# A hybrid decoder layer: the samples' token tile with high and low parts side by side, jobs moved two tiles ahead, and two unread matmuls behind each row of 1/rms

## The chip, the core and the metric

The kernel runs on one core of one Trainium2 chip. The metric is device time in microseconds. Five engines of the core appear in the text: TensorE (PE, with its weight loads PEld), VectorE (DVE), ScalarE (ACT), GpSimd (POOL) and SyncE (SP), which issues most of the DMAs. PSUM, which TensorE writes, is used in banks of 512 fp32 columns.

## The reference

One decoder layer is run for a prompt of 1024 tokens and for 8 sequences of 8 sample tokens (64 samples), with the same weights, 1024 model columns and fp32 data. Cut to the parts that matter here:

```python
def layer(x, ...):
    h = rmsnorm(x, norm_mix)                       # x / sqrt(mean(x*x) + EPS) * g
    q, k, v, gu, gv, ga, gb = split_in(h @ w_in)   # 1024, 256, 256, 768, 768, 1024, 1024 columns
    o, nk, nv = attn_prompt(...) or attn_sample(...)     # window of 128
    vn = layernorm(jax.nn.gelu(gv), ln_g, ln_b)
    s = spatial_gating(jax.nn.gelu(gu), vn, ws, bs)
    merged = jax.nn.sigmoid(ga) * (o @ w_pa) + jax.nn.sigmoid(gb) * (s @ w_pb)
    x = x + merged @ w_out
    f, nconv = conv_ffn(rmsnorm(x, norm_ffn), w_up, conv_w, conv_b, w_down, conv_prev)
    return x + f, nk, nv, nconv, vn
```

A final RMSNorm follows. This text is about the first tenth of the run: h, and of the projection the columns of v and gv.

## The kernel before

**Split numbers.** Every fp32 operand of a large product is split into a high part, which fp32r holds exactly, and a low part, the rest (`split`, L39; `scale_split`, L43, which also scales by the norm's gains). A product is hi·hi + hi·lo + lo·hi: three matmuls into one PSUM bank for each of eight chunks (k) of 128 model columns. A split is a ScalarE copy (L40, L44) and a VectorE subtraction (L41, L45).

**Tokens.** They stand in two groups. Group 0 holds the tile "s" of the 64 samples and the prompt's tiles 0 to 3 (576 tokens), group 1 tiles 4 to 7 (512 tokens). In the first stage, the token stage, the tokens' h is the stationary operand (128 rows of it) and 256 columns of the weights are the moving one, so that the result has tokens as rows: `mm_tok` (L527, matmul L531), 24 matmuls a tile. The samples' tile takes 128 rows as well: 64 samples and the first 64 of prompt tile 0, whose results nobody reads there.

**Order of the token stage.** There are four blocks of 256 columns: gv0, gv1, gv2 and v. Their weights (`w2h`, `w2l`) have two buffers. First comes gv0 for group 0, chunk by chunk as x and weights arrive, into five banks (120 matmuls). Then `tokens` (L570) runs through whole tiles: gv1, v and gv2 for group 0, five tiles each, then v, gv2, gv0 and gv1 for group 1, four tiles each: 31 tiles of 24 matmuls. After that the other columns are computed with weights stationary and tokens moving (`product`, L290, matmul L300), 288 tokens at a time for group 0 and 256 for group 1. These are the products that fill the middle of the run.

**1/rms.** Group 0's h is used without 1/rms, which is applied to the results by row (`rstg`, L537 and L567). The sum of squares by column, `rsg`, is made by ScalarE's squares (L616, L645, L648) and VectorE's additions (L618, L637). `stats` (L470) adds it up over the partitions with fp32 matmuls of one column (L475), takes the root (`rroot`, L255: VectorE, then POOL), and spreads it on diagonals (L482 on ScalarE, L484 on VectorE). `rows` (L486) turns the diagonals into rows by fp32 matmuls with ones (L492) and copies them to `rsg` (L495). For group 1, 1/rms goes into h itself (`norm1`, L661), for which the rows are needed.

**Jobs.** After each tile `tokens` pops one function of the list `jobs` (L717) and runs it. So the list says behind which tile the work of VectorE and ScalarE for later is written: the rows of group 0, group 1's four pairs of squares (`squares1`), `stats1`, the rows of group 1 with the first of four `norm1`, then the sums and splits that the products need (`sums1`, `sums0`, `split0`). A scheduler then sets the final order on each engine from what depends on what.

**Results and room.** `v_out` (L534) and `gv_out` (L564) take a tile from PSUM through ScalarE (L537, the gelu L567) and send it out; gv goes to a DRAM buffer on ScalarE's DMA queue (L568). Group 0's h stands in the space of `txa[0]`, the split tokens of the products (`h_of`, L517); its part `txa[0][3]` stays free until `split0(3)`. Later the LayerNorm over gv reads each tile back (`ln_load`, L743; `ln_stats`, L754; `ln_out`, L764), the samples' tile with 128 rows like the others.

Of the kernel before, what the change touches and what calls it, by code (L numbers as in the profile page):

```python
# [15 lines left out]
P = 128  # L16
# [18 lines left out]
def layer(tc, a):  # L35
# [11 lines left out]
    with ExitStack() as top:  # L47
# [310 lines left out]
        with ExitStack() as ph1:  # L358
# [108 lines left out]
            def bank():  # L467
                return psa.tile([P, 512], F32, name="st")

            def stats(g):  # L470

                acc, n = rsg[g], groups[g]["n"]
                pt = (bank() if g else bank5[4])[:, 256:256 + len(groups[g]["toks"])]
                for i, (_, lo) in enumerate(groups[g]["toks"]):
                    PE.matmul(pt[:, i:i + 1], acc[:, lo:lo + P], ones[:, 0:1], start=True, stop=True)  # L475
                rroot(rstg[g], pt)

                dg = stage(n)
                for i, (name, lo) in enumerate(groups[g]["toks"]):
                    m = NS if name == "s" else P  # L480
                    if g:
                        S.activation(dg[0:m, lo:lo + m], ident[0:m, 0:m], AF.Copy, scale=rstg[g][0:m, i:i + 1])  # L482
                    else:
                        V.tensor_scalar(dg[0:m, lo:lo + m], ident[0:m, 0:m], rstg[g][0:m, i:i + 1], None, ALU.mult)  # L484

                def rows():  # L486
                    ps, at = None, 512
                    for name, lo in groups[g]["toks"]:
                        m = NS if name == "s" else P
                        if at + m > 512:  # L490
                            ps, at, lo0 = bank(), 0, lo
                        PE.matmul(ps[:, at:at + m], ones[0:m], dg[0:m, lo:lo + m], start=True, stop=True)  # L492
                        at += m
                        if at + P > 512 or lo + m == n:
                            S.copy(acc[:, lo0:lo + m], ps[:, :at])  # L495
                return rows

            pa0, th0, pa = ExitStack(), ExitStack(), ExitStack()
# [28 lines left out]
            def mm_tok(ps, g, lo, w, k):  # L527
                wh, wl = w
                ah, al = ((part1(t, k, lo) for t in txa[1][k % 4]) if g else (t[:, lo:lo + P] for t in hs[k]))
                for i, (u, v) in enumerate(((ah, wh), (ah, wl), (al, wh))):  # L530
                    PE.matmul(ps, u, v[:, k, :], start=k + i == 0,  # L531
                              stop=k == KD - 1 and i == 2)

            def v_out(g, i, ps):  # L534
                name = groups[g]["toks"][i][0]
                v = gvp.tile([P, 256], F32, name="gv")
                S.activation(v, ps, AF.Copy, scale=1.0 if g else rstg[g][:, i:i + 1])  # L537
                if name == "s":
                    nc.sync.dma_start(vsd, v[0:NS])
                    for b in range(8):  # L540
                        nc.sync.dma_start(a["vsn"][b], v[8 * b:8 * b + 8])
                else:
                    if name == 4:
                        late["v"] = gvp.tile([P, 256], F32, name="gv")
                        nc.sync.dma_start(late["v"], v3d)
                    for to, x in ((vd, v), (dvd, None)):
                        if x is None and name == 0:
                            continue
                        t = W.sm.tile([P, 4, P], F32, name="ws", bufs=2)
                        tr, four = t.bitcast(F32R), lambda y: y.rearrange("p (h d) -> p h d", d=64)  # L550
                        if x is None:
                            x = t[:, :, 64:128]
                            V.tensor_sub(x, four(v), four(late["v"]))
                            scale_split(tr[:, :, 0:64], tr[:, :, 64:128], x, sign)
                        else:
                            split(tr[:, :, 0:64], tr[:, :, 64:128], four(x))
                        nc.sync.dma_start(to[name], t)
                    late["v"] = v
                    if name == 3:
                        nc.sync.dma_start(v3d, v)  # L560
                if name == 7:
                    nc.sync.dma_start(a["vp"], v)

            def gv_out(g, i, p3, ps, v=None):  # L564
                if v is None:
                    v = gvp.tile([P, 256], F32, name="gv")
                S.activation(v, ps, AF.Gelu_apprx_tanh, scale=1.0 if g else rstg[g][:, i:i + 1])  # L567
                nc.scalar.dma_start(gvd[groups[g]["toks"][i][0]][:, 256 * p3:256 * p3 + 256], v)  # L568

            def tokens(g, key, out, jobs, new=True, after=None):  # L570
                if new:
                    W.get()
                    W.get()
                for i, (_, lo) in enumerate(groups[g]["toks"]):
# [168 lines left out]
            def ln_load(n):  # L743
                if n < len(lnn):
                    if "lnp" not in late:
                        lnp = late["lnp"] = poola("ln", 1, lno)
                        for x in ("lng", "lnb"):
                            late[x] = lnp.tile([P, GW], F32, name=x)
                            nc.sync.dma_start(late[x], a[x])
                    g, i = lnn[n]  # L750
                    lnv[n] = late["lnp"].tile([P, GW], F32, name="v", bufs=4)
                    nc.sync.dma_start(lnv[n], gvd[groups[g]["toks"][i][0]])

            def ln_stats(n):  # L754
                lnp, v = late["lnp"], lnv[n]
                bs_ = lnp.tile([P, 2, 6], F32, name="bst", bufs=2)
                for e in range(2):
                    V.bn_stats(bs_[:, e], v[:, e * 384:e * 384 + 384])
                mv = lnm[n] = lnp.tile([P, 3], F32, name="mv", bufs=3)
                V.bn_aggr(mv[:, 0:2], bs_)  # L760
                V.tensor_scalar(mv[:, 2:3], mv[:, 1:2], EPS, None, ALU.add)
                G.tensor_tensor(mv[:, 2:3], mv[:, 2:3], mhalf[:, 0:1], ALU.pow)

            def ln_out(n):  # L764
                (g, i), v, mv = lnn[n], lnv.pop(n), lnm.pop(n)
                V.scalar_tensor_tensor(v, v, mv[:, 0:1], late["lng"], ALU.subtract, ALU.mult)
                V.scalar_tensor_tensor(v, v, mv[:, 2:3], late["lnb"], ALU.mult, ALU.add)
                nc.sync.dma_start(vnd[g][:, :, i], v.rearrange("p (g c) -> p g c", c=P))
                if groups[g]["toks"][i][0] == "s":
                    nc.sync.dma_start(a["gvs"], v[0:NS])  # L770

            def ln_half(n, e):
                def go():
# [1227 lines left out]
```

## Time and profile before

| | |
|---|---|
| median of 3 runs | 1510.91 us (1510.36 to 1510.93) |
| profiled execution | 1509.93 us, of which the span is 1508.2 |
| granted TensorE clock | 0.998 |
| TensorE busy | 1493.7 us, 99% of the span, 12190 matmuls |
| VectorE, ScalarE, POOL busy | 1158.7 (77%), 825.9 (55%), 265.8 (18%) us |
| first product of the next stage | at 112.44 us |

A timeline row of the trace gives start, time covered, engine, line, operation, result<-operands, partitions, shapes and how many instructions follow one another in it; a time in brackets at its end is the engine's idle time before it and what ended it. A matmul's time covered is longer than its distance to the next one, since they are pipelined; the distance is read from the starts. A row of a window gives the window, its length, then busy time and count for TensorE, its loads, VectorE, ScalarE and POOL, then clock, DMA share and GB/s. Rows of the engines' order have no times: they give line, operation, result<-operands and the count of equal ones in a row.

### The profile page before, as it was taken

Reading aid. Unit: us, or ns where it says so; the run is one execution under the profiler, and the core shown is the slowest. Engines: PE = TensorE matmul, PEld = TensorE weight load, DVE = VectorE, ACT = ScalarE, POOL = GpSimd, SP = SyncE. Lnnn points to the kernel's source line nnn. Section 1 sums busy time; section 2 is a strip of 40 time slices with the busy share of each in tenths; the row PEclk is TensorE's granted clock in tenths of the full one; section 3 lists DMA queues with packets and bytes.
Section 4 is the critical chain, followed back from the end, with each engine's and each line's share of the span. In section 5 each row is a group of like instructions: output and inputs, shape, how many; then the busy total and the mean of one; then the engine's idle time right before and its main releaser. Section 6 shows DMA issues by size and latency. Waiting matters only on the chain.

```text
span 1508.2 us, 31375 instructions
## 1 busy us (share of the span) xinstructions
PE 1493.7 (99%) x12190; PEld 1481.7 (98%) x12190; DVE 1158.7 (77%) x1909; ACT 825.9 (55%) x1755; POOL 265.8 (18%) x422
## 2 busy tenths in 40 slices
PE   9999999999999999999999999999999999999997
PEld 9999999999999999999999999999999999999997
DVE  6896778756645995989668888898899888785685
ACT  6665764544543774874434555555555556453463
POOL 0000012200120331530222322322132122000002
PEclk9999999999999999999999999999999999999999
DMA  8452457637749757849978333332233226973453
GB/s 289 157 188 112 179 177 265 228 126 271 243 167 333 249 181 224 254 160 322 342 257 282 129 115 122 117 117 107 98 136 109 91 74 219 367 259 97 123 183 133
DMA packets 137508, 286.70 MB, mean 190 GB/s; under 512 B 15248, under 2 KB 44368, under 8 KB 137360
## 3 DMA queue, kind: packets, MB, share of 16 engines
q1 hardware_dynamic: 132352, 279.97, 55.2%
q10 hardware_dynamic: 5008, 4.73, 0.9%
q8 instruction: 96, 1.57, 0.4%
q14 instruction: 52, 0.43, 0.1%
HBM read 195.76 MB, written 90.85 MB: 190 GB/s over the span
## 4 chain that ended last, share of the span: by engine, by line
PE 76%; DVE 5%; ACT 2%; issue 1%; DMA 1%; POOL 0%; DVEq 0%; ACTq 0%; POOLq 0%
PE st L300 41%; PE dn L1740 15%; PE mm L240 14%; PE sc L1233 1%; PE mx L841 1%; PE po L1294 1%; ACT s L1256 1%; DVE s L1259 1%; DVE s L1243 1%; DVE nm L1249 1%; PE pt L1266 1%; DVE of L1305 0%; DVE wl L41 0%; DVE pl L41 0%; DMA v<-gvd 0%
## 5 line engine op out<-in xcount | busy, mean ns | idle before, releaser
L300 PE MATMUL st<-th,wh 128*128 128x256 f32 (+1 forms) x2128 | 610.6, 287 | 1.2 <-ACT ku L283 0.8
L300 PE MATMUL st<-tl,wh 128*128 128x256 f32 (+1 forms) x2128 | 608.7, 286 | 0.0
L300 PE MATMUL st<-th,wl 128*128 128x256 f32 (+1 forms) x2128 | 608.2, 286 | 0.0
L300 PEld LDWEIGHTS st<-th,wh 128*128 128x128 f32 x2128 | 399.9, 188 | 2.6 <-ACT k L281 1.2
L300 PEld LDWEIGHTS st<-th,wl 128*128 128x128 f32 x2128 | 400.3, 188 | 0.0
L300 PEld LDWEIGHTS st<-tl,wh 128*128 128x128 f32 x2128 | 399.7, 188 | 0.0
L40 ACT CAST wh<-wraw 128x512 fp32r<-128x512 f32 (+2 forms) x204 | 139.4, 694 | 99.7 <-PE st L300 35.3
L41 DVE TENSOR_TENSOR wl<-wraw,wh 128x512 fp32r<-128x512 f32 (+2 forms) x204 | 158.5, 790 | 40.2 <-ACT wh L40 38.3
L1740 PE MATMUL dn<-th,wh 128*128 128x288 f32 (+1 forms) x616 | 176.7, 287 | 0.0
L1740 PE MATMUL dn<-tl,wh 128*128 128x288 f32 (+1 forms) x616 | 176.2, 286 | 0.0
L1740 PE MATMUL dn<-th,wl 128*128 128x288 f32 (+1 forms) x616 | 175.1, 284 | 0.0
L40 ACT CAST wh<-ws 128x512 fp32r<-128x512 f32 x160 | 98.1, 622 | 99.8 <-PE st L300 65.5
L41 DVE TENSOR_TENSOR wl<-ws,wh 128x512 fp32r<-128x512 f32 x160 | 111.1, 707 | 44.1 <-ACT wh L40 42.1
L1740 PEld LDWEIGHTS dn<-th,wl 128*128 128x128 f32 x616 | 115.8, 188 | 0.0
L1740 PEld LDWEIGHTS dn<-tl,wh 128*128 128x128 f32 x616 | 115.7, 188 | 0.0
L1740 PEld LDWEIGHTS dn<-th,wh 128*128 128x128 f32 x616 | 115.6, 188 | 0.0
L288 POOL TENSOR_TENSOR z<-ku,k 128x256 f32<-128x256 f32 (+1 forms) x32 | 29.5, 926 | 316.7 <-ACT ku L283 315.4
L41 DVE TENSOR_TENSOR tl<-traw,th 128x544 fp32r<-128x544 f32 (+1 forms) x85 | 61.4, 730 | 22.9 <-ACT th L40 22.8
L40 ACT CAST th<-traw 128x544 fp32r<-128x544 f32 (+1 forms) x85 | 53.8, 642 | 43.9 <-PE dn L1740 28.6
L240 PE MATMUL mm<-s,wh 128*128 128x256 f32 (+1 forms) x384 | 76.7, 294 | 0.0
L531 PE MATMUL st<-w2h,th 128*128 128x256 f32 x308 | 74.5, 283 | 0.2 <-DVE w2l L165 0.2
L240 PE MATMUL mm<-oh,wh 128*128 128x256 f32 (+1 forms) x256 | 73.5, 288 | 0.2
(300 smaller groups left out, 3157.9 us busy)
## 6 DMA issues: line engine op xcount, KB each, us to landing
wraw<-wt SPq DMA_DIRECT2D x133, 512.0 KB
traw<-td SPq DMA_DIRECT2D x77, 272.0 KB
td<-za SPq DMA_DIRECT2D x22, 544.0 KB
wraw<-wt SPq DMA_DIRECT2D x35, 256.0 KB
upd<-hl SPq DMA_DIRECT2D x14, 512.0 KB
td<-t SPq DMA_DIRECT2D x11, 544.0 KB
qd<-q SPq DMA_DIRECT2D x8, 576.0 KB
q<-qd SPq DMA_DIRECT2D x8, 576.0 KB
```

The costliest lines, as they stand in the source:

```text
L40: S.copy(hi, src)
L41: V.tensor_sub(lo, src, hi.bitcast(F32))
L240: PE.matmul(ps[:, lo:lo + c1 - c0], u[:, k, :], v[:, c0:c1], start=(clear and k == 0 and i == 0), stop=(k == nk - 1 and i == 2), skip_grou ...
L288: op(to, pick(x, to, lo, hi), pick(y, to, lo, hi))
L300: PE.matmul(ps, u[:, kk, :], v, start=first and kk + i == 0, stop=kk == 3 and i == 2, skip_group_check=True)
L531: PE.matmul(ps, u, v[:, k, :], start=k + i == 0, stop=k == KD - 1 and i == 2)
L841: PE.matmul(ps[:, P * i:P * i + P], vn[:, i], late["wst"][:, c, :], start=True, stop=True)
L1233: PE.matmul(ps[:, h, o0:256], q, kst[kv][:, e, k0:cur + P], start=e == 0, stop=e == 1)
L1243: V.copy_predicated(s[:, :, 0:P], late["mprev"].to_broadcast([P, 4, P]), ps[:, :, 0:P])
L1249: V.tensor_reduce(nm, s, AX.X, ALU.max, negate=True)
L1256: S.activation(s[:, h], s[:, h], AF.Exp, bias=nm[:, h:h + 1], accum_out=dn[:, h:h + 1])
L1740: PE.matmul(place(m, e), u[:, m, :], v[:, lo:hi], start=new and i + k == 0 and (e == 0 or m % 2 == 0), stop=i == NU - 1 and k == 2, skip_g ...
```

## The change

It has five parts.

1. **Pair tile.** Sixteen POOL copies (L649 after) put the samples' 64 high parts and 64 low parts of each chunk side by side in 128 columns, `pair_s`, in the free `txa[0][3]`.
2. **Samples' tile.** For gv1, v and gv2 it uses `pair_s` against the high and the low weights: 16 matmuls (L601 after) in place of 24. Rows 0 to 63 of the result come from the high parts and 64 to 127 from the low ones; `joined` adds them with a ScalarE copy (L542) and a VectorE addition (L543). The product lo·lo, which was left out, is now in it.
3. **Jobs.** `squares1` starts behind gv1's first tile, and everything from `stats1` on stands two tiles sooner.
4. **Unread matmuls.** Behind the last L492 of each group stand two matmuls with 288 moving columns (L500 after) of a high weight tile and h of the samples, into a bank that nobody reads. `issue_after` keeps them behind that L492.
5. **Outputs.** The samples' tile is written and read back with 64 rows, in the LayerNorm too.

```diff
-                        PE.matmul(ps[:, at:at + m], ones[0:m], dg[0:m, lo:lo + m], start=True, stop=True)
+                        end = PE.matmul(ps[:, at:at + m], ones[0:m], dg[0:m, lo:lo + m], start=True, stop=True)
...
+                    with tc.issue_after(end.ins):
+                        idle = bank()[:, 0:288]
+                        x = wide[("gv1", "v")[g]][0].rearrange("p k c -> p (k c)")[:, 0:288]
+                        for i in range(2):
+                            PE.matmul(idle, hs[0][0][:, 0:P], x, start=True, stop=True, skip_group_check=True)
...
+            def joined(ps):
+                t = gvp.tile([P, 256], F32, name="gv")[0:NS]
+                S.copy(t, ps[NS:P])
+                V.tensor_add(t, t, ps[0:NS])
+                return t
...
             def v_out(g, i, ps):
-                v = gvp.tile([P, 256], F32, name="gv")
-                S.activation(v, ps, AF.Copy, scale=1.0 if g else rstg[g][:, i:i + 1])
+                if name == "s":
+                    v = joined(ps)
+                    S.activation(v, v, AF.Copy, scale=rstg[g][0:NS, i:i + 1])
...
             def gv_out(g, i, p3, ps, v=None):
+                m = NS if name == "s" else P
+                if name == "s" and p3:
+                    v = ps = joined(ps)
...
-                nc.scalar.dma_start(gvd[groups[g]["toks"][i][0]][:, 256 * p3:256 * p3 + 256], v)
+                nc.scalar.dma_start(gvd[name][0:m, 256 * p3:256 * p3 + 256], v[0:m])
...
                     for k in range(KD):
-                        mm_tok(ps, g, lo, wide[key], k)
+                        if name != "s":
+                            mm_tok(ps, g, lo, wide[key], k)
+                            continue
+                        for e in range(2):
+                            PE.matmul(ps, pair_s[:, k], wide[key][e][:, k, :], start=k + e == 0,
+                                      stop=k == KD - 1 and e == 1)
...
+            pair_s = txa[0][3][0].rearrange("p j c -> p (j c)")[:, 0:KD * P].rearrange("p (k c) -> p k c", c=P)
+            for k, x in enumerate(hs):
+                for e in range(2):
+                    G.tensor_copy(pair_s[:, k, 64 * e:64 * e + 64], x[e][:, 0:NS])
...
-            jobs = [none, none, lambda: rows[0](), *(squares1(kk) for kk in range(4)), stats1,
+            jobs = [squares1(0), squares1(1), both(lambda: rows[0](), squares1(2)), squares1(3), none, stats1,
                     both(lambda: rows[1](), norm1(0)), *(norm1(kk) for kk in range(1, 4)),
...
             def ln_load(n):
-                    lnv[n] = late["lnp"].tile([P, GW], F32, name="v", bufs=4)
-                    nc.sync.dma_start(lnv[n], gvd[groups[g]["toks"][i][0]])
+                    m = NS if groups[g]["toks"][i][0] == "s" else P
+                    lnv[n] = late["lnp"].tile([P, GW], F32, name="v", bufs=4)[0:m]
+                    nc.sync.dma_start(lnv[n], gvd[groups[g]["toks"][i][0]][0:m])
```

`ln_stats` and `ln_out` use the same 64 rows for the samples' tile.

The engines' order shows it at two places. The first is TensorE around group 1's 1/rms. `w2h` and `w2l` are the high and low weights, th_245 and tl_246 the last chunks of group 0's h, th_237 its first. Before, at the end of the fourth v tile and the start of the fifth:

```order
L531 MATMUL st<-w2h,th_245 128x256 x2
L531 MATMUL st<-w2l,th_245 128x256
L531 MATMUL st<-w2h,tl_246 128x256
L492 MATMUL st<-stg,c_ones 128x128 x4
L531 MATMUL st<-w2h,th_237 128x256
```

Now, at the end of the second v tile and the start of the third:

```order
L536 MATMUL st<-w2h,th_245 128x256 x2
L536 MATMUL st<-w2l,th_245 128x256
L536 MATMUL st<-w2h,tl_246 128x256
L492 MATMUL st<-stg,c_ones 128x128 x4
L500 MATMUL st<-w2h,th_237 128x288 x2
L536 MATMUL st<-w2h,th_237 128x256
```

The four L492 moved ahead by two tiles, and two matmuls of 288 columns stand behind them. The sums over the partitions (L475) moved with them, from behind the third v tile to behind the first; one whole tile lies between L475 and L492 in both kernels.

The second is ScalarE's queue in gv1. The squares of group 1 are stg<-wh (L648 before, L677 now), the gelus are L567 and L587, and L568 and L588 send gv to DRAM. Before, from the copies of group 0's rows on:

```order
L495 COPY rs_217<-st 128x448
L495 COPY rs_217<-st 128x128
L648 ACTIVATE stg<-wh 128x512 x2
L567 ACTIVATE gv<-st,rst_219 128x256
L648 ACTIVATE stg<-wh 128x512
L568 DMA gvd_153<-gv 128x256
L648 ACTIVATE stg<-wh 128x512 x3
L567 ACTIVATE gv<-st,rst_219 128x256
```

Now, from gv1's second gelu to its fifth:

```order
L677 ACTIVATE stg<-wh 128x512
L587 ACTIVATE wl<-st,rst_219 128x256
L495 COPY rs_217<-st 128x448
L588 DMA gvd_152<-wl 128x256
L495 COPY rs_217<-st 128x128
L677 ACTIVATE stg<-wh 128x512 x2
L587 ACTIVATE gv<-st,rst_219 128x256
L677 ACTIVATE stg<-wh 128x512
L588 DMA gvd_153<-gv 128x256
L677 ACTIVATE stg<-wh 128x512
L587 ACTIVATE gv<-st,rst_219 128x256
```

Before, six of the squares stood behind the rows of group 0 in this piece and the seventh later, behind the first v tile; now three stand ahead of the rows, and all seven stand ahead of the fifth gelu.

More of the change, by code (lines that the diff above doesn't have):

```diff
@@ L532, in mm_tok @@
                               stop=k == KD - 1 and i == 2)
+            def joined(ps):
[3 more added lines that the diff above has]
+                return t
             def v_out(g, i, ps):
                 name = groups[g]["toks"][i][0]
-                v = gvp.tile([P, 256], F32, name="gv")
-                S.activation(v, ps, AF.Copy, scale=1.0 if g else rstg[g][:, i:i + 1])
+                if name == "s":
+                    v = joined(ps)
+                    S.activation(v, v, AF.Copy, scale=rstg[g][0:NS, i:i + 1])
+                else:
+                    v = gvp.tile([P, 256], F32, name="gv")
+                    S.activation(v, ps, AF.Copy, scale=1.0 if g else rstg[g][:, i:i + 1])
                 if name == "s":
@@ L573, in tokens @@
                     W.get()
-                for i, (_, lo) in enumerate(groups[g]["toks"]):
+                for i, (name, lo) in enumerate(groups[g]["toks"]):
                     ps = bank()[:, :256]
                     for k in range(KD):
-                        mm_tok(ps, g, lo, wide[key], k)
+                        if name != "s":
[4 more added lines that the diff above has]
+                                      stop=k == KD - 1 and e == 1)
                     if after and i == 0:
@@ L750, in ln_load @@
                     g, i = lnn[n]
-                    lnv[n] = late["lnp"].tile([P, GW], F32, name="v", bufs=4)
-                    nc.sync.dma_start(lnv[n], gvd[groups[g]["toks"][i][0]])
+                    m = NS if groups[g]["toks"][i][0] == "s" else P
+                    lnv[n] = late["lnp"].tile([P, GW], F32, name="v", bufs=4)[0:m]
+                    nc.sync.dma_start(lnv[n], gvd[groups[g]["toks"][i][0]][0:m])
             def ln_stats(n):
                 lnp, v = late["lnp"], lnv[n]
-                bs_ = lnp.tile([P, 2, 6], F32, name="bst", bufs=2)
+                m = v.shape[0]
+                bs_ = lnp.tile([P, 2, 6], F32, name="bst", bufs=2)[0:m]
                 for e in range(2):
                     V.bn_stats(bs_[:, e], v[:, e * 384:e * 384 + 384])
-                mv = lnm[n] = lnp.tile([P, 3], F32, name="mv", bufs=3)
+                mv = lnm[n] = lnp.tile([P, 3], F32, name="mv", bufs=3)[0:m]
                 V.bn_aggr(mv[:, 0:2], bs_)
                 V.tensor_scalar(mv[:, 2:3], mv[:, 1:2], EPS, None, ALU.add)
-                G.tensor_tensor(mv[:, 2:3], mv[:, 2:3], mhalf[:, 0:1], ALU.pow)
+                G.tensor_tensor(mv[:, 2:3], mv[:, 2:3], mhalf[0:m, 0:1], ALU.pow)
             def ln_out(n):
                 (g, i), v, mv = lnn[n], lnv.pop(n), lnm.pop(n)
[L766 to L770, printed above, removed]
+                m = v.shape[0]
+                V.scalar_tensor_tensor(v, v, mv[:, 0:1], late["lng"][0:m], ALU.subtract, ALU.mult)
+                V.scalar_tensor_tensor(v, v, mv[:, 2:3], late["lnb"][0:m], ALU.mult, ALU.add)
+                nc.sync.dma_start(vnd[g][0:m, :, i], v.rearrange("p (g c) -> p g c", c=P))
+                if m == NS:
+                    nc.sync.dma_start(a["gvs"], v)
             def ln_half(n, e):
```

5 lines of the change are left out of this document (3 added, 2 removed).

## The prediction

> **What bounds the kernel now.** I read the page first, then TensorE's waits, then the starts of its matmuls in the stage that the change touches. The page's head, with span, busy time, share and count:
>
> ```profile
> span 1508.2 us, 31375 instructions
> PE 1493.7 (99%) x12190; PEld 1481.7 (98%) x12190; DVE 1158.7 (77%) x1909; ACT 825.9 (55%) x1755; POOL 265.8 (18%) x422
> ```
>
> TensorE is busy for 99% of the span, so what the change does to its queue counts in full, and what it does elsewhere counts where TensorE comes to wait. Its waits in the token stage (5.2 to 112.4 us) are these (total, times, longest):
>
> ```profile
> PE st L531 <- ACT tl L44: 0.6, 1, 0.6
> PE st L531 <- DVE w2l L165: 0.2, 1, 0.2
> ```
>
> After the start nothing is waited for there. Busy time says nothing of how far apart matmuls start, so next come the starts themselves: TensorE's timeline in this stage (start, time covered, instruction), at its breaks.
>
> ```profile
> 32.15 0.28 PE L531 MATMUL st<-w2l,th 128*128 128x256 f32 x1
> ...
> 45.64 0.95 PE L475 MATMUL st<-c_ones,rs 128*128 128x1 f32 x8
> 46.45 0.36 PE L531 MATMUL st<-w2h,th 128*128 128x256 f32 x1
> ...
> 49.36 1.05 PE L492 MATMUL st<-stg,c_ones 128*128 128x128 f32 x8
> 50.17 0.36 PE L531 MATMUL st<-w2h,th 128*128 128x256 f32 x1
> 50.37 0.28 PE L531 MATMUL st<-w2l,th 128*128 128x256 f32 x1
> ...
> 112.44 0.28 PE L300 MATMUL st<-th,wh 128*128 128x256 f32 x1
> ```
>
> Between 32.15 and 45.64 lie 119 matmuls (five tiles of 24, without the first): 13.49 / 119 = 0.1134 us each. Between 50.37 and 112.44 lie 527: 62.07 / 527 = 0.1178. They are the same instructions of the same shape with no wait; the spacing changed at the short fp32 matmuls of group 1's 1/rms (L475) and stayed so. The first products (L300) begin in the slow spacing too. Elsewhere a run of 288 columns before one of 256 is followed by the quick one, here in the products:
>
> ```profile
> 137.13 0.29 PE L300 MATMUL st<-th,wh 128*128 128x288 f32 x1
> ...
> 137.93 0.28 PE L300 MATMUL st<-th,wh 128*128 128x256 f32 x1
> ...
> 138.40 0.28 PE L300 MATMUL st<-tl,wh 128*128 128x256 f32 x1
> ...
> 138.96 0.28 PE L300 MATMUL st<-th,wh 128*128 128x256 f32 x1
> ```
>
> Six of 288 take 0.80 (0.133 each), the next four of 256 0.47 (0.118), and the five after those 0.56 (0.112). So two 288s should lead back to the quick spacing within some four matmuls.
>
> **The change, part by part.** *Fewer matmuls.* Three samples' tiles (gv1, v, gv2 of group 0) fall from 24 to 16: 24 x 0.1134 = 2.72 us. Nothing hides these, so they come off the end.
>
> *The spacing.* TensorE's order (section on the change) shows L492 two tiles further ahead than before, with two 288s behind it. Before, 24 + 528 = 552 matmuls ran slowly; now only the 24 between L475 and L492 should. At 0.1178 - 0.1134 = 0.0044 us, 528 x 0.0044 = 2.32. The products before 115 us, about 24, start quickly too: 0.1. The four new matmuls cost 4 x 0.133, and the four after each pair lag by 4 x (0.118 - 0.1134) = 0.02: 0.57 lost. Together 2.72 + 2.32 + 0.10 - 0.57 = 4.57 us gained, if TensorE never waits more than it did.
>
> [...]
>
> *The copies on POOL.* Sixteen 128x64 copies build the pair tile. What they meet is VectorE, whose busy time from 10.0 to 21.2 us is 11.10 of 11.20 (TensorE, its loads, then VectorE, ScalarE, POOL):
>
> ```profile
> 10.00:21.20 11.20, 10.79 (x91) 10.51 (x91) 11.10 (x16) 10.08 (x16) 0.00 (x0) 1.00 1.01 340
> ```
>
> TensorE is released by VectorE here: its split of chunk 4 ends at 13.73 + 0.81 = 14.54 and that of the gv1 weights at 21.20 (VectorE's timeline), and TensorE starts on them at 14.60 and 21.48 (its own):
>
> ```profile
> 13.73 0.81 DVE L45 SCALAR_TENSOR_TENSOR tl<-wh,c_gains,th 128x576 fp32r<-128x576 f32 x1
> ...
> 18.85 2.35 DVE L41 TENSOR_TENSOR w2l<-wraw,w2h 128x1024 fp32r<-128x1024 f32 x2
> ```
>
> ```profile
> 14.60 0.39 PE L531 MATMUL st<-w2h,tl 128*128 128x256 f32 x1
> ...
> 21.29 0.35 PE L531 MATMUL st<-w2l,th 128*128 128x256 f32 x1
> 21.48 0.40 PE L531 MATMUL st<-w2h,th 128*128 128x256 f32 x2
> ```
>
> So whatever VectorE loses until 21.2, TensorE loses. The nearest rows are sixteen small POOL copies (L913; min, median, max ns), and VectorE's starts beside them against starts without POOL:
>
> ```profile
> L913 POOL COPY qs<-stg x16: 229/234/742, 439.2 to 445.1; 64x64 f32<-64x64 f32 x16
> ```
>
> ```profile
> 109.96 0.69 DVE L41 TENSOR_TENSOR wl<-ws,wh 128x512 fp32r<-128x512 f32 x1
> 110.56 0.68 DVE L41 TENSOR_TENSOR wl<-wraw,wh 128x512 fp32r<-128x512 f32 x1
> ...
> 441.54 0.69 DVE L41 TENSOR_TENSOR wl<-wraw,wh 128x512 fp32r<-128x512 f32 x1 [3.06 <-ACT wh L40]
> 442.32 0.69 DVE L41 TENSOR_TENSOR wl<-ws,wh 128x512 fp32r<-128x512 f32 x1
> 443.05 0.69 DVE L179 TENSOR_TENSOR ws<-ws,wraw 128x512 f32<-128x512 f32 x1
> ```
>
> Alone the next start comes after 0.60, beside the copies after 0.78 and 0.73: 0.13 to 0.18 lost per copy. The first four copies fall where VectorE still has gaps, so twelve count. Ends: nothing, where a copy slips between two operations, and 12 x 0.234 = 2.8 us, if VectorE stood still for each. I take 0.09 (midway between nothing and 0.18): 1.1 us. No gain is to be had here. POOL itself hides the copies: they have from 17.4 (the last split) to 21.3.
>
> *Jobs two tiles sooner.* This adds no wait by itself, but the sum of squares must now be ready two tiles earlier. In ScalarE's order three squares now stand ahead of the rows of group 0, and the last of the seven is done before gv1's fifth gelu. Their prices, on ScalarE and VectorE:
>
> ```profile
> 28.09 0.84 ACT L567 ACTIVATE wl<-st,rst 128x256 f32<-128x256 f32 x2 [0.53 <-ACT wl L567]
> ...
> 29.45 0.84 ACT L567 ACTIVATE wl<-st,rst 128x256 f32<-128x256 f32 x2 [0.52 <-ACT wl L567]
> ...
> 32.01 1.05 ACT L40 CAST w2h<-wraw 128x1024 fp32r<-128x1024 f32 x1
> ...
> 32.96 0.69 ACT L495 COPY rs<-st 128x448 f32<-128x448 f32 x2
> 33.54 1.17 ACT L648 ACTIVATE stg<-wh 128x512 f32<-128x512 f32 x2
> ...
> 37.16 1.68 ACT L648 ACTIVATE stg<-wh 128x512 f32<-128x512 f32 x3 [1.20 <-DMA gvd<-wl]
> ```
>
> ```profile
> 42.44 0.68 DVE L637 TENSOR_TENSOR rs<-rs,stg 128x512 f32<-128x512 f32 x1
> ```
>
> Counted from the first gelu (I put it at 26.9): three pairs of gelus with their issues at 29.45 - 28.09 = 1.36, seven squares at 0.56, three gelus at 0.4, a cast, two copies and three issues at 0.4 come to about 12, so the last square ends near 38.9 and its add near 39.6. TensorE comes to L475 at 32.15 - 0.9 + 1.1 + 0.3 + 48 x 0.1134 + 16 x 0.1134 = 39.9. That is a tie where before there were 45.64 - 43.12 = 2.5 us to spare. Bounds: nothing, and the 1.20 that ScalarE once waits for a landing of gvd; I take 0.2, nearest to the tie. The chain from L475 to L492 has one tile for itself, as before. The joins (a ScalarE copy and a VectorE add for each of the three tiles) cost under 0.5 us each off TensorE's path, ahead of a bank that is wanted five tiles later.
>
> Behind this, VectorE must keep up (stages by windows, same columns):
>
> ```profile
> 51.00:66.00 15.00, 15.00 (x130) 15.00 (x129) 14.92 (x30) 8.90 (x19) 0.00 (x0) 1.00 0.33 123
> ...
> 96.00:111.00 15.00, 15.00 (x129) 15.00 (x129) 14.88 (x25) 9.10 (x19) 0.00 (x0) 1.00 0.39 117
> ...
> 126.00:236.00 110.00, 110.00 (x883) 110.00 (x882) 78.59 (x120) 73.38 (x147) 8.55 (x10) 1.00 0.49 175
> 237.00:277.00 40.00, 39.10 (x313) 38.62 (x312) 39.17 (x76) 17.91 (x38) 13.12 (x12) 1.00 0.79 262
> ```
>
> From 51 to 111 it is nearly full, but its chain starts at the rows of 1/rms, which come some 5 to 6 us sooner while TensorE ends the stage only 3 to 4 sooner; so it gains on TensorE. After 126 it has a quarter to spare. At 237 to 277 (LayerNorm) TensorE already waits 0.9; all that is set off by the products, and moves with them. The smaller LayerNorm tile of samples changes free sizes nowhere: nothing.
>
> *Sum.* 4.57 - 1.1 - 0.2 = 3.3 us. The profiled execution took 1509.93 us (its span 1508.2 and 1.73 around it): 1506.6. The median of the runs shown is 0.98 above it, so 1507.6, a gain of 0.22%. About 0.2%, 3.0 us, is what can be told from no change here.
>
> **The rivals.** *The copies stop VectorE for their whole length.* For it: VectorE has no gap to give. Against: beside L913 it lost 0.13 to 0.18, not 0.23. Price 2.8, and 0.4 at L475: 4.57 - 3.2 = 1.4, 1509.5. The Trainium skill ("SBUF — State Buffer", section "Who interferes with whom") says that a VectorE instruction with two SBUF inputs and a GpSimd one that reads SBUF exclude each other, the second waiting for the whole of the first; the L913 rows agree in kind, and show half the length lost.
>
> *The spacing doesn't come back* (the unread matmuls don't do what they would have to): another stationary or bank is at work than in the products. 24 x 0.1178 - 0.57 - 1.1 - 0.2 = 1.0: 1509.9. [...] Against: the products show the return each time that I looked, with the same shapes.
>
> *Slower: L475 comes before its input.* If the sum of squares is ready no sooner than it was (43.12), TensorE stands for 3.4 us at L475, and if ScalarE is then held by another landing as at 37.16, L492 waits 1.2 more: 3.3 + 0.2 - 4.6 = -1.1, so 1512.0. It decides from 3.5 us of lateness. For it: ScalarE's own queue holds the DMA issues that wait. Against: seven squares sooner in the queue.
>
> **How the numbers follow.** Forecast 0.52 (1505.8 to 1507.9: copies between nothing and 0.13 each); whole-length copies 0.20 (to 1509.9); spacing not back 0.14 (1509.9); L475 early 0.14, of which 0.06 beyond 3 us of loss. Faster by over 0.2%: 0.52; within: 0.42; slower: 0.06. The range 1505.6 to 1510.8 leaves out those 0.06 and some 0.08 at the ends.
>
> **What would show it.** In the profile after: samples' tiles of 16 matmuls; 0.1134 us from the second 288 to the first product; gv1 starting at 22 to 23 instead of 21.48; a wait of TensorE at L475 under 0.5 us; the first product near 109. I am wrong if the spacing stays at 0.1178, if VectorE loses over 0.2 per copy, or if the first product's lead is gone by 280 us.

## The result and the profile after

The changed kernel takes 1513.07 us (median of 22 runs, 1510.0 to 1516.74), the kernel before 1510.72 (22 runs beside them, 1509.0 to 1513.03). The ratio is 1.0017, with an interval of 1.0011 to 1.0023: slower by 0.17%, clear of the noise of so many runs, where 3.3 us of gain were forecast. The profiled execution's span is 1510.5 us, 2.3 longer than before:

```profile
PE 1492.9 (99%) x12170; PEld 1480.6 (98%) x12170; DVE 1158.9 (77%) x1912; ACT 827.5 (55%) x1758; POOL 277.8 (18%) x438
```

TensorE has the 20 matmuls less that were counted (24 saved, 4 added), but is busy only 0.8 us less, and it waits more. Its waits from 30 to 125 us, where before it had none:

```profile
PE st L300 <- ACT k L281: 2.2, 1, 2.2
PE st L475 <- DVE rs L666: 0.6, 1, 0.6
```

TensorE's timeline at the places that the prediction named:

```profile
21.33 0.28 PE L601 MATMUL st<-w2h,th 128*128 128x256 f32 x1
...
23.22 1.17 PE L475 MATMUL st<-c_ones,rs 128*128 128x1 f32 x10
...
39.52 1.05 PE L475 MATMUL st<-c_ones,rs 128*128 128x1 f32 x8 [0.58 <-DVE rs L666]
...
43.35 1.29 PE L492 MATMUL st<-stg,c_ones 128*128 128x128 f32 x8
44.40 0.51 PE L500 MATMUL st<-w2h,th 128*128 128x288 f32 x2
44.74 0.28 PE L536 MATMUL st<-w2h,th 128*128 128x256 f32 x1
...
111.65 0.28 PE L300 MATMUL st<-th,wh 128*128 128x256 f32 x1
...
116.76 0.38 PE L300 MATMUL st<-th,wh 128*128 128x256 f32 x1 [2.22 <-ACT k L281]
```

gv1 starts at 21.33, no later than before (21.48). From 44.74 to 111.65 lie 568 matmuls: 66.91 / 568 = 0.1178, still the slow spacing, behind two 288s. So the first product stands at 111.65 instead of 112.44: 0.8 gained in place of 3.3. Then, 24 products on, TensorE waits 2.2 us for the copy of a product's bank (L281). ScalarE's timeline there:

```profile
110.05 0.37 ACT L587 ACTIVATE gv<-st 128x256 f32<-128x256 f32 x1
...
111.76 0.39 ACT L587 ACTIVATE gv<-st 128x256 f32<-128x256 f32 x1 [0.46 <-PE st L536]
112.04 0.61 ACT L40 CAST th<-stg 128x512 fp32r<-128x512 f32 x1
...
112.55 1.66 ACT L40 CAST th<-stg 128x512 fp32r<-128x512 f32 x3
115.56 0.38 ACT L587 ACTIVATE gv<-st 128x256 f32<-128x256 f32 x1 [1.35 <-DMA gvd<-gv]
...
116.34 0.65 ACT L281 COPY k<-st 128x256 f32<-128x256 f32 x2 [0.40 <-ACT gv L587]
```

The last gelu waits for one of the three gv buffers, and the copy for which TensorE waits stands behind it. Before, the last gelu came right behind the same casts, with no wait for a buffer, and TensorE's 25th product started without one either:

```profile
114.09 0.38 ACT L567 ACTIVATE gv<-st 128x256 f32<-128x256 f32 x1
```

```profile
115.29 0.39 PE L300 MATMUL st<-th,wh 128*128 128x256 f32 x1
```

The buffer for which the last gelu now waits is that of the tile sent at 110.45. The chain of waits shows its landing, and an earlier one (start, time):

```profile
85.06 5.22 DMA gvd<-gv
...
110.45 5.02 DMA gvd<-gv
```

Before, ScalarE also waited for landings of gv, and TensorE never had to wait for it in this stage:

```profile
ACT gv L567 <- DMA gvd<-gv: 2.8, 1, 2.8
ACT th L40 <- DMA gvd<-gv: 1.3, 1, 1.3
```

Now it waits 5.3:

```profile
ACT gv L587 <- DMA gvd<-gv: 5.3, 3, 2.9
```

### The profile page after: what moved, and what is told of

Its sections match the earlier page's. It is cut to its first block, busy times and chain, and to the rows that moved or that the text cites. A ratio compares the mean times of both kernels' runs of the same rounds, so it can differ in the third digit from the quotient of the medians.

```text
span 1510.5 us, 31362 instructions
## 1 busy us (share of the span) xinstructions
PE 1492.9 (99%) x12170; PEld 1480.6 (98%) x12170; DVE 1158.9 (77%) x1912; ACT 827.5 (55%) x1758; POOL 277.8 (18%) x438
## 4 chain that ended last, share of the span: by engine, by line
PE 85%; DVE 8%; ACT 2%; DMA 2%; issue 2%; POOL 0%; ACTq 0%; SPq 0%; DVEq 0%; POOLq 0%
PE st L300 49%; PE dn L1772 15%; PE mm L240 15%; PE sc L1265 1%; DMA gvd<-gv 1%; DVE tl L41 1%; PE po L1326 1%; PE mx L873 1%; PE st L536 1%; DVE wl L41 1%; ACT s L1288 1%; PE pt L1298 1%; DMA dvd<-ws 0%; DVE s L1275 0%; DVE nm L1281 0%
## 5 line engine op out<-in xcount | busy, mean ns | idle before, releaser
L240 PE MATMUL mm<-ol,wh 128*128 128x256 f32 (+1 forms) x256 | 73.7, 288 | 0.0
```

What stands on the lines that cost most here:

```text
L240: PE.matmul(ps[:, lo:lo + c1 - c0], u[:, k, :], v[:, c0:c1], start=(clear and k == 0 and i == 0), stop=(k == nk - 1 and i == 2), skip_grou ...
```

## The experiments

Thirteen runs followed; e12 is the changed kernel again. Those of one group below shared a chip and the runs of the kernel before. "Landings" is what ScalarE waited for landings of gv between 40 and 120 us, "stage" what TensorE waited between 40 and 125, "behind L492" the spacing after group 1's rows of 1/rms; these three are from one profiled execution each, in us. That execution need not be typical: those of e3 and e9 are their fastest (1506.84 and 1505.59), that of e8 is its second slowest (1517.26). The ratio is not the quotient of the two medians: where a kernel's times are spread unevenly, as e1's (8 of 12 from 1508.5 to 1509.4, 4 from 1512.3 to 1514.7), the two differ, and it is the ratio that counts.

| kernel | median, of before | ratio (interval) | landings | stage | behind L492 |
|---|---|---|---|---|---|
| before | | | 4.1 | 0 | 0.1178 |
| changed | 1513.07, 1510.72 | 1.0017 (1.0011 to 1.0023) | 5.3 | 2.2 | 0.1178 |
| e1 more gv buffers | 1509.16, 1511.22 | 0.9999 (0.9989 to 1.0008) | 0 | 1.3 | 0.1133 |
| e2 one narrow | 1515.66, 1511.22 | 1.0019 (1.0009 to 1.0029) | 4.4 | 4.1 | 0.1133 |
| e3 narrow and buffers | 1509.58, 1511.22 | 0.9991 (0.998 to 1.0001) | 0 | 0.9 | 0.1133 |
| e4 no unread | 1510.98, 1511.22 | 0.9995 (0.9987 to 1.0004) | 4.8 | 2.2 | 0.1133 |
| e5 before, buffers | 1510.99, 1512.23 | 0.9994 (0.9985 to 1.0003) | 3.1 | 0 | 0.1178 |
| e6 jobs as before | 1513.76, 1512.23 | 1.0006 (0.9994 to 1.0018) | 5.4 | 3.6 | 0.1133 |
| e7 buffers, sums later | 1508.88, 1512.23 | 0.9981 (0.9968 to 0.9994) | 2.4 | 0 | 0.1178 |
| e8 no pair tile | 1514.23, 1512.23 | 1.0008 (0.9998 to 1.0019) | 7.2 | 3.8 | 0.1133 |
| e9 e7 and 288s | 1507.13, 1512.39 | 0.9969 (0.9959 to 0.9979) | 0.3 | 0 | 0.1133 |
| e10 e7 and one narrow | 1507.10, 1512.39 | 0.9969 (0.9955 to 0.9983) | 0.4 | 0 | 0.1133 |
| e11 e7 and two narrow | 1508.83 (one run) | | 0.3 | 0 | 0.1178 |
| e12 changed again | 1514.01, 1512.39 | 1.001 (1.0001 to 1.0019) | 4.7 | 3.9 | 0.1133 |
| e13 e9 without buffers | 1508.10, 1511.41 | 0.9977 (0.9967 to 0.9987) | 1.4 | 0 | 0.1133 |

**First group: buffers and spacing.** The theory after the first trace: the spacing goes by the passes that stand before it, and the wait at the products comes of the landing of gv.

```diff
 e1, in gv_out
-                    v = gvp.tile([P, 256], F32, name="gv")
+                    v = rsg[1][:, 128 * (i - 1):128 * (i - 1) + 256] if g and i % 2 else gvp.tile([P, 256], F32, name="gv")
 e2, in rows; e3 is both; e4 has neither this nor the unread matmuls
-                        idle = bank()[:, 0:288]
-                        x = wide[("gv1", "v")[g]][0].rearrange("p k c -> p (k c)")[:, 0:288]
-                        for i in range(2):
-                            PE.matmul(idle, hs[0][0][:, 0:P], x, start=True, stop=True, skip_group_check=True)
+                        idle = bank()[:, 0:P]
+                        x = dg[0:m, lo:lo + m]
+                        for i in range(1 * g):
+                            PE.matmul(idle, ones[0:m], x, start=True, stop=True, skip_group_check=True)
```

> The changed kernel, with every second gv tile of group 1 written into the sums of squares of group 1 (two tiles' room, free by then) instead of the three gv buffers. Theory: TensorE's new wait of 2.5 us at the products' start (L300, 116.76) is the last gelu waiting for the landing of the gv tile sent at 110.45; with more room the last gelu runs right behind ScalarE's casts, at about 114.2, and the wait falls by at least 1.3 us, the time with it: 1511.0 to 1511.8. The spacing from 44 to 111 us stays 0.1178. Rival: the wait is ScalarE's and VectorE's late work for the products, whatever the buffers; then it stays at 2.4 and the time at 1513.

> The changed kernel, without the four unread matmuls of 288 columns; in place of group 1's pair, one unread fp32 matmul of 128 columns (a repeat of the last L492, two passes). In the traces the spacing is quick after ten fp32 passes in a row (group 0's L475 and L492) and slow after eight (group 1's), whatever it was before and with or without 288s behind. Theory: the count of passes decides, so ten at L492 bring 0.1134 from 44 us on, and the first product comes at about 109 instead of 111.65; TensorE then waits longer at the products for ScalarE, so that the time stays near 1512.5 to 1513. Rival 1: which spacing follows is chance of the execution; then 0.1178 stays as often as not. Rival 2: only a wider matmul resets; then 0.1178 stays, first product at 111.

> Both of the two edits before. Theory: first product near 109 with 0.1134 from 44 us, and TensorE's wait at the products about 3 us or less, since VectorE's splits for the products still end near 114; the time 1509.5 to 1511. If the landing of gv was all that held ScalarE, 1508. Rival (chance or width sets the spacing): as the kernel with more gv buffers, 1511.0 to 1511.8.

> The changed kernel without its four unread matmuls. Theory: they did nothing for the spacing: quick between group 0's 1/rms and group 1's, slow from there on, as with them; the four save 0.6 us, which shows at the first product (111.0) and is lost in the wait behind it: 1512.4 to 1513.1. Rival: group 0's pair did its work (the spacing between 31 and 39 us was quick behind it); then that stretch runs at 0.1178 here, 0.3 us longer.

With room (e1, e3) ScalarE's waits for landings of gv are gone, and TensorE's wait at the products falls to 1.3 and 0.9 us. What is left of it is ScalarE's own row behind the last tiles: four casts, the last gelu and the copy. The medians of e1 and e4 (1509.16 and 1510.98) lie below their forecasts, that of e3 (1509.58) inside. e4 came out otherwise than expected: without the unread matmuls the kernel is no slower than before (0.9995), although ScalarE waits 4.8 us and TensorE 2.2 in its trace. So the four unread matmuls came with more than the 0.57 us reckoned for them; how, no run shows. All four traces have the quick spacing behind L492, where the theory forecast the slow one for e1 and e4: e4 has nothing unread at all, and e1 has the changed kernel's order on TensorE. So what sets the spacing could not be told from this group. e2 is the sharpest: TensorE was over 2 us ahead, and lost it twice.

```profile
PE st L300 <- ACT k L281: 2.2, 1, 2.2
PE st L536 <- DVE w2l L41: 1.9, 1, 1.9
```

The second row is a new place: the wide weights' split, behind a wait of ScalarE of 3.4 us for a landing. The time, forecast near 1513, was 1515.66. Behind that wait the spacing was 0.1177 again. The quick spacing up to there bought nothing.

**Second group: parts of the change.**

```diff
 e5: the line of e1 in the kernel before
 e6: the jobs of before in the changed kernel
 e7: no unread matmuls, the line of e1, and
-            jobs = [squares1(0), squares1(1), both(lambda: rows[0](), squares1(2)), squares1(3), none, stats1,
+            jobs = [squares1(0), squares1(1), both(lambda: rows[0](), squares1(2)), squares1(3), none, none, stats1,
 e8: the samples' tile by mm_tok again, without pair_s and joined
```

> The kernel before, with every second gv tile of group 1 written into group 1's sums of squares (the two tiles more room of the earlier run, without any part of the change). Theory: before, ScalarE stands 2.8 and 1.3 us for landings too (at 87.8 and 69 us), but TensorE needs nothing of it in time, since it waits 0.1 us at the products; so the room takes ScalarE's waits away and moves the time by less than 1 us (1510 to 1511.2). Rival: the room helps whatever the change does, and its gain in the changed kernel (from 1513.1 to 1509.2) says nothing of the change; then 1509 or less here.

> The changed kernel with the list of jobs of before. Theory: the 0.6 us wait of TensorE at L475 goes, but the rows of 1/rms come two tiles later, and VectorE, full from there to the products, starts its list some 5 us later while TensorE ends the stage about as soon; TensorE waits over 3 us at the products or for split weights, and the time is 1512 to 1514. Rival: the two tiles bring nothing, since ScalarE's landings set the products' start; then as the changed kernel without its wait at L475, 1512.4 or less, with a wait of 2.4 as now.

> The changed kernel without the unread matmuls, with the two tiles more room for gv, and with the sums of group 1's squares one tile later than now (one sooner than before). Theory: no wait at L475 (0.7 to 0.9 less), none of ScalarE for a landing of gv, the first product at 107.5 with the quick spacing (110 with the slow one), and 3 to 4 us from the last tile to the copy of the first product: 1507 to 1508.5 by the quick spacing, up to 1510 by the slow one. Rival: VectorE's list, begun one tile later, is late for the products by the same tile; then 1510 in either spacing.

> The changed kernel with the samples' tile as before: 24 matmuls, no pair tile, no copies on POOL, no joins (its outputs still of 64 rows). What is left are the jobs two tiles sooner and the unread matmuls. Theory: TensorE ends the stage 2.7 us later than the changed kernel in the same spacing, ScalarE's chain keeps its distance to the last tile (4.7 us with a landing wait, 2.4 as before without), so the wait at the products stays 1 to 2.5: 1513 to 1515.5. Rival: ScalarE and VectorE are what ends late in the changed kernel, whatever TensorE does; then TensorE meets them just in time, as before, and the time is 1511 to 1512.

e5: more room does nothing measurable for the kernel before, as the theory had it, though ScalarE still waited 3.1 us for landings there. e6 keeps the pair tile: TensorE, early, waits 3.6 us for split weights, and the time is what the theory gave. e8 keeps the jobs two tiles sooner and not the pair tile: with no fewer matmuls, TensorE waits 3.8 us in both places, and the forecast of 1513 to 1515.5 held. So the jobs' shift makes waits without the pair tile, as the pair tile does without the shift (e6); neither part alone is the cause. e7, sums one tile later, has no wait at L475, none at the products, and is faster than before.

**Third group: what sets the spacing.** e9, e10 and e11 are e7 with group 1's pair of 288s, with one narrow fp32 matmul, and with two.

```diff
 e9, in rows
-                        for i in range(2):
+                        for i in range(2 * g):
 e10 as e2; e11 as e2 with range(2 * g)
```

> The version with more room, no unread matmuls and the sums one tile later, which ran at 0.1178 from group 1's L475 on, with the two unread matmuls of 288 columns put back behind group 1's L492 alone. There L492 ran without a wait for its diagonals (109 ns from the last token matmul); in the changed kernel it waited between its passes (up to 182 ns). Theory: behind an L492 without waits the pair brings the quick spacing back, as in the run with the old jobs: 0.1134 from 45 us, the first product 2.0 to 2.3 us sooner (107.2), the time 1506.5 to 1507.3. Rival: the pair does nothing and chance decides: 0.1178 as likely as not, then 1509.

> The same version with one unread fp32 matmul of 128 columns (ten passes in a row) behind group 1's L492 in place of the pair of 288s. Theory: ten passes leave the quick spacing behind them, eight the slow one (so it stood in every trace behind an L475 or L492 that had no wait in it), so 0.1134 from 45 us, first product at 107.2, 1506.5 to 1507.3. Rival: the count means nothing; 0.1178 as likely as not, 1509.

> The same with two unread fp32 matmuls of 128 columns, twelve passes in a row. If the spacing goes by the count in fours (eight slow, ten quick), it is slow again: 0.1178, first product at 109.5. If ten or more do, it is quick, first product at 107.4. Which of the two, no run so far says; I lean to the first (0.6).

> The changed kernel once more, unaltered, for a second trace. Theory: L475's wait (0.5 to 0.9), the landing waits of ScalarE (about 5 us in all) and TensorE's wait for the first products' bank (over 1.5 us) come again; behind group 1's L492, which waits between its passes, the spacing may be either one. Time 1512 to 1514, above the kernel before by 1.5 us or more. Rival: what the first trace shows was that execution's own; then the waits differ, and the median is that of the kernel before.

TensorE's timelines, first e7 (eight passes):

```profile
44.45 1.05 PE L492 MATMUL st<-stg,c_ones 128*128 128x128 f32 x8
45.26 0.36 PE L536 MATMUL st<-w2h,th 128*128 128x256 f32 x1
...
109.41 0.28 PE L300 MATMUL st<-th,wh 128*128 128x256 f32 x1
```

e9 (eight passes and the pair):

```profile
44.53 1.05 PE L492 MATMUL st<-stg,c_ones 128*128 128x128 f32 x8
45.34 0.51 PE L500 MATMUL st<-w2h,th 128*128 128x288 f32 x2
45.69 0.28 PE L536 MATMUL st<-w2h,th 128*128 128x256 f32 x1
...
107.36 0.28 PE L300 MATMUL st<-th,wh 128*128 128x256 f32 x1
```

e10 (ten passes):

```profile
44.22 1.05 PE L492 MATMUL st<-stg,c_ones 128*128 128x128 f32 x8
45.11 0.39 PE L500 MATMUL st<-stg,c_ones 128*128 128x128 f32 x2
45.25 0.37 PE L536 MATMUL st<-w2h,th 128*128 128x256 f32 x1
...
107.01 0.28 PE L300 MATMUL st<-th,wh 128*128 128x256 f32 x1
```

e11 (twelve passes):

```profile
44.64 1.05 PE L492 MATMUL st<-stg,c_ones 128*128 128x128 f32 x8
45.53 0.61 PE L500 MATMUL st<-stg,c_ones 128*128 128x128 f32 x4
45.89 0.36 PE L536 MATMUL st<-w2h,th 128*128 128x256 f32 x1
...
110.05 0.28 PE L300 MATMUL st<-th,wh 128*128 128x256 f32 x1
```

From the first token matmul behind L492 to the first product there are 544: 0.1179 each in e7, 0.1134 in e9, 0.1135 in e10, 0.1179 in e11. In all four L492 takes 1.05 us, its passes in one go. Behind eight passes in one go the spacing was slow in three traces of three (before, e5, e7), and with the pair behind them quick in three of three (e6, e9, e13): there the pair does what it was put in for. That ten passes leave the quick spacing and twelve the slow one stands on one trace each (e10, e11). In the changed kernel L492 takes 1.29, since its passes wait for ScalarE's diagonals; there no rule holds: the quick spacing followed in e1, e2, e3, e4, e8 and e12, whatever stood behind L492, and the slow one in the first trace. e12, the same kernel again (L492 1.36), got 0.1133 where the first trace had 0.1178. And its time was no better: TensorE spent the gain in two waits.

```profile
PE st L300 <- ACT k L281: 2.5, 1, 2.5
PE st L536 <- DVE w2l L41: 1.4, 1, 1.4
```

**Last: room or order?** e7 and e9 had two edits at once. e13 is e9 with gv in its three buffers again (the line of e1 undone).

> The fastest version so far (sums one tile later, group 1's unread pair alone), with the two tiles more room for gv taken away: the changed kernel with one none more in its jobs and without group 0's pair. Theory: ScalarE's waits for landings of gv, 0.3 us with the room, come back to 4 us or more, and TensorE waits 1.5 us or more for split weights near 98 us or for the first product's bank; time 1510 to 1512. Rival: the order that the one tile gives (diagonals ready in one go, the last gelu ahead of the stage's end) took the wait at the products away, and the room is not needed: no wait of TensorE above 0.5 in the stage, 1507 to 1508.5.

The rival was right. Without the room ScalarE waits 1.4 us for landings of gv and TensorE not at all in the stage; 1508.10 against 1511.41. So the order that the one tile gives is enough without more buffers, and my reading that the kernel needs more room fell; what room adds to it (0.9969 in e9, 0.9977 in e13) is within the intervals. e13 also lacks group 0's unread pair, but that takes neither the wait nor the time with it: e4 lacks both pairs, still waits 2.2 us and is at 0.9995. Part of what the order does shows in the DMA issues. In the changed kernel SyncE issues two loads of 512 KB (L146) around the gv tile of 85.06 (the row covers both; the second is issued at 85.33) and one beside that of 110.45:

```profile
83.86 1.80 SPq L146 DMA_DIRECT2D wraw<-wt  x2
...
110.46 0.33 SPq L146 DMA_DIRECT2D wraw<-wt  x1
```

In e13 the loads and the gv tiles of ScalarE's queue alternate:

```profile
80.44 0.33 SPq L146 DMA_DIRECT2D wraw<-wt  x1
...
83.84 0.43 SPq L146 DMA_DIRECT2D wraw<-wt  x1
```

```profile
82.73 0.33 ACTq L588 DMA_DIRECT2D gvd<-gv  x1
86.59 0.33 ACTq L588 DMA_DIRECT2D gvd<-gv  x1
```

That a gv tile lands late because it was sent among such loads is read from these rows; no run moved a load alone. The order around 85 us isn't new either: before, the loads went out at 83.53 and 85.00 and the gv tile at 85.04, and the gelu behind it waited 2.8 us as well. So this order is not what tells the changed kernel from the one before; that TensorE comes sooner for what stands behind it is, and that is argued, not tested.

## Why the prediction was wrong

**The step that failed** is the cover. The prediction said that the chain behind the rows of 1/rms starts 5 to 6 us sooner, "so it gains on TensorE", and looked at VectorE's share alone. VectorE did start sooner: L492 stands 6.0 us earlier (43.35, before 49.36), and from 45 to 51 VectorE is busy 5.62 us, where before it was 1.41. From 90 to 100 it lost 1.6 of that: 7.07 busy, before 8.67 (first the two rows of before, then of after).

```profile
45.00:51.00 6.00, 6.00 (x55) 6.00 (x54) 1.41 (x4) 3.48 (x9) 1.02 (x1) 1.00 0.54 180
...
90.00:100.00 10.00, 10.00 (x87) 10.00 (x87) 8.67 (x15) 6.89 (x14) 0.00 (x0) 1.00 0.60 187
```

```profile
45.00:51.00 6.00, 6.00 (x54) 6.00 (x53) 5.62 (x10) 3.48 (x8) 0.00 (x0) 1.00 0.48 155
...
90.00:100.00 10.00, 10.00 (x88) 10.00 (x87) 7.07 (x11) 6.38 (x12) 0.00 (x0) 1.00 0.37 126
```

In that stretch ScalarE stood at a gelu for a landing, and VectorE for ScalarE's casts behind it (a row of each):

```profile
90.37 0.38 ACT L587 ACTIVATE gv<-st 128x256 f32<-128x256 f32 x1 [2.90 <-DMA gvd<-gv]
```

```profile
91.86 0.76 DVE L41 TENSOR_TENSOR tl<-wl,th 128x576 fp32r<-128x576 f32 x1 [2.58 <-ACT th L40]
```

At the products nothing was left of the lead. VectorE began their splits at 112.66 before and begins them at 112.68 now, having waited 1.05 us for ScalarE's casts:

```profile
112.66 2.50 DVE L41 TENSOR_TENSOR tl<-stg,th 128x512 fp32r<-128x512 f32 x4 [0.21 <-ACT th L40]
```

```profile
112.68 2.50 DVE L41 TENSOR_TENSOR tl<-stg,th 128x512 fp32r<-128x512 f32 x4 [1.05 <-ACT th L40]
```

ScalarE works in order and is busy just over half the time, so its share showed no limit. What it waits for did, and stood in the trace of before (4.1 us for landings). A list of what ScalarE waits for in the stage, with the distance to TensorE's next need, would have shown that 3 us of lead were not covered. The rival on landings placed them at L492 only, too early. In the profiled execution the miss has two parts of like size: 2.5 us ahead of the first product, where the spacing stayed slow, and 2.2 in the wait behind it. That the second is enough by itself is shown by e12: with the quick spacing it waits 3.9 us and is slower than before as well.

**Fewer matmuls, 2.72.** Right: the first samples' tile takes 23.22 - 21.33 = 1.89 for 16.

**The spacing, 2.32 and 0.1.** The mechanism holds where L492 runs in one go: e9 has its first product 2.05 us ahead of e7's. The prediction took it to hold always; behind an L492 that waits, the pair was followed by the quick spacing in e1, e8 and e12 and by the slow one in the first trace, and e4 has the quick one there without any pair. That was the term lost in the first trace: 568 matmuls at 0.0044 us are 2.5.

**Unread matmuls, 0.57.** About right for their own time: 44.74 - 44.40 = 0.34 for a pair. What e4 saved beyond it was not in the sum.

**Copies, 1.1.** Mis-sized: they cost nothing that shows. VectorE's steps near 15 us start 0.66 and 0.73 us apart beside them (before 0.67 and 0.73), and it comes to the gv1 weights at 18.84 (before 18.85). It was the copies that stretched, from 0.24 to 0.7 us (L649; min, median, max ns):

```profile
L649 POOL CAST th<-th x9: 232/677/784, 4.0 to 18.1; 128x64 fp32r<-128x64 f32 x9
```

```profile
18.84 2.38 DVE L41 TENSOR_TENSOR w2l<-wraw,w2h 128x1024 fp32r<-128x1024 f32 x2
```

The rule of the Trainium skill ("SBUF — State Buffer", section "Who interferes with whom") that one engine waits for the whole of the other's instruction agrees with the copies' length; but beside a busy VectorE it was POOL that waited, so the rival built on it fell. (The rows of L913 showed 0.13 to 0.18 of 0.234 us lost, which is more than half the length.)

**L475, 0.2 (0 to 1.2).** In the bounds: 0.58, and 0.3 in e12. The sum was ready at 39.5, as forecast (39.6); TensorE came at 38.9 and not at 39.9, since the copies had cost it nothing. The wait goes with one tile (e7, e9, e13).

**The sum.** At the same product, the 25th, TensorE stood at 116.76 and, before, at 115.29: 1.47 of the 2.3 us. In the rest of the run its waits for product banks (L281, L283) are 0.5 longer, but other waits (L1265, before L1233) are as much shorter, so the last 0.8 is not accounted for. Nor is the stage all that sets a time: e1 and e4 come to the 25th product at 113.35 and 113.49, 1.9 and 1.8 us sooner than the kernel before, and are no faster (0.9999 and 0.9995). From that product to the end the traces take from 1392.5 us (e3) to 1398.0 (e2 and e8), of which the half clock behind the stage is 1.6 in e2 and e8; what makes the rest of this difference is not known.

**The rivals.** "Spacing not back" came true in the first trace, but the time that it gave (1509.9) has no wait at the products in it. "Slower" had the right side and the wrong place: L475 cost 0.58, not 3.4. The chance of 0.06 for slower was too small, for it counted landings at one place and not at the many where ScalarE's queue can meet them.

What stays open: how the unread matmuls cost what e4 saves, what the time behind the 25th product depends on, why the same order of instructions leaves the quick or the slow spacing when L492 waits, and what in the executions of the kernel before makes its spread (1508.8 to 1517.0 on one chip).

## What to carry to other kernels

When the engine that bounds a kernel is made faster by a few microseconds, list for every in-order engine that feeds it what that engine waits for, not how busy it is: a queue that stands 4 us for landings is covered only as long as nobody needs it sooner. Move such work by the smallest step and measure each: here one tile sooner is 0.23% faster (e13, without group 0's pair), and two tiles sooner 0.17% slower. And work that is put in to change an engine's pace, as the unread pair here, should stand behind work that runs without waits: behind an L492 that waited it was followed by the quick pace in three traces and by the slow one in one.

## What the runs showed of the hardware

**Spacing of matmuls.** The same 128x256 fp32r matmuls ran at 0.1133 or 0.1178 us and kept to one of them for hundreds (568 at 0.1178 in the changed kernel, 544 at 0.1134 in e9). Behind eight narrow fp32 passes in one go it was slow (before, e5, e7), in one trace each slow behind twelve (e11) and quick behind ten (e10). It also changed elsewhere: at the first product of the changed kernel from 0.1178 to 0.1135 with nothing waited for, and in e2 from 0.1133 to 0.1177 behind a wait of 1.9 us, while such waits in e8 and e12 left it quick.

**The clock.** In e2 TensorE came out of its wait of 2.2 us at half the clock, for 3.4 us (TensorE, loads, VectorE, ScalarE, POOL, granted clock):

```profile
116.00:119.40 3.40, 3.40 (x16) 3.40 (x17) 0.00 (x0) 0.56 (x2) 0.00 (x0) 0.50 0.11 39
```

Sixteen matmuls in 3.4 us, 0.213 each, cost about 1.6 us on top of the wait. From 119.4 on the granted clock is 1.00 again. e8 lost as much behind its wait of 1.9 us at the products, and e6 behind one of 2.6 for split weights. Behind the changed kernel's wait of 2.2 and e12's of 2.5 the products ran on at 0.11 to 0.13 us. The Trainium skill ("TensorE: Matmul & The Clock Gate", section "Part 1: The HAM clock gate") gives half rate after an idle window of about 3.4 us that runs free of the kernel. The stretch at half rate has the length of that window, but here waits of 1.9 to 2.6 us were enough, in three cases of eight.
